# Attention weights turned by VectorE blocks and transfers through DRAM, and memory softmax ahead of the gate

## The chip, the cores and the metric

The kernel runs on one core of a Trainium2 chip. Its metric is the device time of one execution in microseconds (us). The engines named here are TensorE (PE: matmuls and transposes; PEld is its loading of the stationary operand), VectorE (DVE), ScalarE (ACT), GpSimd (POOL) and SyncE (SP). SP and POOL each issue transfers on a queue of their own. SBUF is the memory beside the engines, PSUM the one into which PE writes, DRAM the large memory outside.

## The reference, cut to what matters

Four layers, whose mixers are latent attention, sparse attention, sliding window and latent attention again. Sequence 256, width 2048. Every layer also has four memory heads of dimension 256 over a memory of 256 rows. The part that the change touches is the softmax weight `p` on its way to the product with `v`:

```
def _mla_branch(...):                       # latent: 16 heads, two blocks of 128 queries
    s = (einsum('bqhd,bkhd->bhqk', qn, k_nope) + einsum('bqhd,bkd->bhqk', qr, k_rope)) * scale
    p = softmax(where(causal, s, NEG_INF)); return einsum('bhqk,bkhd->bqhd', p, v)
def _memory_attention(mq, mem_kv):          # 4 heads
    s = einsum('bqhd,bkhd->bhqk', mq, mk) * MEM_HEAD_DIM ** -0.5
    p = softmax(s); return einsum('bhqk,bkhd->bqhd', p, mv)
def reference(...):                         # per layer
    y = concatenate([self_out, mem_out]) * silu(gate)
    x = x + y @ w_out[i]
```

## The kernel before

All products run in fp32r, in two parts: every operand is split into `hi` (a rounded copy, ACT, L65) and `lo` (what is left, DVE, L74), and a product takes three matmuls (hi hi, lo hi, hi lo). Weights come from DRAM by `stage` on SP's queue (L223, and L227 where columns are picked out of each head) into `wr`, a ring of four tiles; `parts_of` splits them in pieces of 128x512 into `wh` and `wl`, rings of four tiles each. `columns_by` puts the features of the result on partitions (L283 with wh, L287 with wl, a piece is 8 matmuls), `rows_by` the rows of the sequence (L263, L264, L265, a piece is 6 matmuls).

A layer works in six parts, in the order 4, 0, 1, 2, 3, 5. Parts 4 and 5 are two memory heads each (`memory_project`, `memory_attend`), the others are self heads; in the two latent layers a part is four heads (`Latent.project`, `Latent.attend`). After the heads of a part come the products of the part before with `w_out` (`acc_wo`, added to `x` by DVE at L1170). So there are 32 latent heads and 16 memory heads in which the changed functions run.

In such a head the scores lie with queries on partitions. DVE and ACT form the softmax `e` (L546 to L552 in latent heads, where L547 shows as ISA in the order: a custom instruction and the reading of its accumulator), ACT multiplies by the reciprocal of the sum (`normalized`). The product with `v` needs keys on partitions: `weights_T` turns `e` in blocks of 128x128 on PE (L524) into the PSUM tile `ptp`, three blocks for a latent head (causal: the upper right one is zero), four for a memory head. `split` makes `pT` hi and lo of it, and L534 and L535 (`attend`) or L612 (`memory_attend`) multiply.

What sets the order: the program is written head after head, and a scheduler with a simulated timeline orders each engine's list when the kernel is built; each engine then runs its list strictly in that order and waits on semaphores. The splits of the weights have a higher priority by 1000 places (`tc.high_priority`). Instructions of the heads stand between those of the surrounding products, so that PE has weights to multiply while DVE and ACT form a softmax. POOL's queue carries the transfers between DRAM and SBUF that aren't weights: `mkr` and `mvr` (keys and values of memory heads), `xm`, the bias tables (`tab`, `bm`) and, towards the end, pieces of `w_out` that are split ahead (`hl`, `sw`, `wk`).

## Time and profile before

| what | value |
|---|---|
| time, median of 3 runs | 2548.99 us (2548.82 to 2549.72) |
| the profiled execution's own time | 2549.14 us |
| its span, first to last instruction | 2547.4 us |
| granted TensorE clock, mean | 0.999 |
| busy: PE / DVE / ACT / POOL | 2534.6 / 1906.2 / 1605.9 / 115.6 us |
| data moved | 515.84 MB, mean 202 GB/s |

The span is what the trace covers, from the first to the last instruction; the time of an execution has a little more around it. Busy shares are averages over the span. Matmul records overlap each other, so a sum of their durations is not PE's time; the distance between starts is. The chain of work is followed back from the last instruction, at each step to what released it. A row of waits gives the engine and line that stood still, what released it, the time in all, the number of times and the longest.

### The profile page before, as it was taken

The page shows a single profiled execution, that of the slowest core. Times are in us where ns is not written, and L with a number is a line of the kernel's source. Part 1 is how long each engine was busy: PE and PEld are TensorE (multiplying, and loading weights), DVE is VectorE, ACT ScalarE, POOL GpSimd, SP SyncE. Part 2 cuts the span into 40 slices and gives each one's busy share as a digit, 9 for nine tenths or more (in the row PEclk, how much of TensorE's full clock was granted, in tenths as well). Part 3 has the DMA queues.
Part 4 walks back from the last instruction along what each step waited for, and adds up shares of the span by engine and source line. Part 5 has one row for each costly group of instructions (what it writes and reads, how often), then busy time and mean ns, then how long its engine had stood idle before and what let it go on. Part 6 is the DMA issues. An engine that isn't in the chain of part 4 may idle for free.

```text
span 2547.4 us, 41829 instructions
## 1 busy us (share of the span) xinstructions
PE 2534.6 (99%) x13928; PEld 2181.2 (86%) x13928; DVE 1906.2 (75%) x4218; ACT 1605.9 (63%) x3480; POOL 115.6 (5%) x274
## 2 busy tenths in 40 slices
PE   9999999999999999999999999999999999999998
PEld 7888888888888889888888888888889888888887
DVE  6666667677777778988787777777878777787776
ACT  6555556566556657667776566766666656665665
POOL 1000000000000000000000010000000000000000
PEclk9999999999999999999999999999999999999999
DMA  8788777666667667666666585666556777676764
GB/s 293 246 266 267 243 218 237 185 166 186 188 175 217 194 203 244 185 201 175 203 182 182 153 258 177 183 177 186 174 172 194 227 205 200 191 194 182 213 180 179
DMA packets 478522, 515.84 MB, mean 202 GB/s; under 512 B 70192, under 2 KB 390592, under 8 KB 477152
## 3 DMA queue, kind: packets, MB, share of 16 engines
q1 hardware_dynamic: 460080, 449.71, 60.6%
q0 software_dynamic: 17504, 62.45, 7.3%
q8 instruction: 110, 1.80, 0.3%
q14 instruction: 108, 0.88, 0.1%
q10 hardware_dynamic: 720, 0.98, 0.1%
HBM read 483.61 MB, written 29.46 MB: 201 GB/s over the span
## 4 chain that ended last, share of the span: by engine, by line
PE 99%; ACT 0%; DVE 0%; DMA 0%; issue 0%; DVEq 0%
PE acc_g L283 14%; PE acc_g L287 7%; PE acc_wo L263 7%; PE acc_wo L264 7%; PE acc_wo L265 7%; PE acc_mq L283 5%; PE acc_q L283 5%; PE acc_mk L283 5%; PE acc_cq L283 4%; PE acc_qn L283 4%; PE acc_mk L287 2%; PE acc_q L287 2%; PE acc_mq L287 2%; PE acc_mv L263 2%; PE acc_mv L264 2%; PE acc_mv L265 2%
## 5 line engine op out<-in xcount | busy, mean ns | idle before, releaser
L74 DVE TENSOR_TENSOR wl<-wr,wh 128x512 fp32r<-128x512 f32 (+1 forms) x1712 | 1154.6, 679 | 545.6 <-ACT wh L65 521.6
L65 ACT ACTIVATE wh<-wr 128x512 fp32r<-128x512 f32 (+1 forms) x1712 | 1060.7, 622 | 775.0 <-PE acc_g L283 160.5
L283 PE MATMUL acc_g<-xT,wh 128*128 128x512 f32 x1536 | 487.3, 397 | 1.1 <-DVE mqT L325 1.1
L287 PEld LDWEIGHTS acc_g<-xT,wl 128*128 128x128 f32 x1536 | 284.0, 188 | 61.7
L287 PE MATMUL acc_g<-xT,wl 128*128 128x256 f32 x1536 | 309.3, 280 | 0.0
L264 PE MATMUL acc_wo<-wl,y 128*128 128x512 f32 x752 | 294.8, 392 | 0.0
L265 PE MATMUL acc_wo<-wh,y 128*128 128x512 f32 x752 | 291.8, 390 | 0.0
L283 PEld LDWEIGHTS acc_g<-xT,wh 128*128 128x128 f32 x1536 | 237.4, 189 | 7.0 <-issue 3.1
L263 PE MATMUL acc_wo<-wh,y 128*128 128x512 f32 x752 | 241.1, 392 | 0.0
L264 PEld LDWEIGHTS acc_wo<-wl,y 128*128 128x128 f32 x752 | 141.3, 188 | 28.8
L265 PEld LDWEIGHTS acc_wo<-wh,y 128*128 128x128 f32 x752 | 141.3, 188 | 28.6
L283 PE MATMUL acc_mq<-xT,wh 128*128 128x512 f32 x512 | 163.1, 397 | 0.0
L263 PEld LDWEIGHTS acc_wo<-wh,y 128*128 128x128 f32 x752 | 139.3, 188 | 27.2 <-ACT wh L65 0.2
L283 PE MATMUL acc_q<-xT,wh 128*128 128x512 f32 x512 | 162.4, 396 | 0.0
L283 PE MATMUL acc_mk<-mT,wh 128*128 128x512 f32 x512 | 161.0, 396 | 0.3 <-ACT wh L65 0.3
L1170 DVE TENSOR_TENSOR x<-x,acc_wo 128x512 f32<-128x512 f32 x184 | 120.6, 680 | 12.0 <-PE acc_wo L265 11.7
L283 PE MATMUL acc_qn<-cT,wh 128*128 128x512 f32 x384 | 121.9, 397 | 0.0
L283 PE MATMUL acc_cq<-xT,wh 128*128 128x512 f32 x384 | 121.0, 396 | 0.0
L287 PEld LDWEIGHTS acc_mk<-mT,wl 128*128 128x128 f32 x512 | 96.0, 188 | 24.1 <-DVE wl L74 1.2
L287 PEld LDWEIGHTS acc_q<-xT,wl 128*128 128x128 f32 x512 | 95.9, 188 | 21.9
L287 PEld LDWEIGHTS acc_mq<-xT,wl 128*128 128x128 f32 x512 | 94.8, 188 | 20.3
L287 PE MATMUL acc_mq<-xT,wl 128*128 128x256 f32 x512 | 103.6, 280 | 0.0
(324 smaller groups left out, 4217.5 us busy)
## 6 DMA issues: line engine op xcount, KB each, us to landing
wr<-in_w_out_dram SPq DMA_DIRECT2D x188, 512.0 KB, 3.7
wr<-in_w_in_a_dram SPq DMA_DIRECT2D x176, 512.0 KB, 4.1
wr<-in_w_mem_kv_dram SPq DMA_DIRECT2D x120, 512.0 KB, 4.8
wr<-in_w_in_b_dram SPq DMA_DIRECT2D x116, 512.0 KB, 3.7
wr<-in_w_in_c_dram SPq DMA_DIRECT2D x104, 512.0 KB, 4.0
wr<-in_w_uq_dram SPq DMA_DIRECT2D x192, 128.0 KB, 2.7
wr<-in_w_uq_dram SPq DMA_DIRECT2D x48, 256.0 KB, 3.4
wr<-in_w_in_a_dram SPq DMA_DIRECT2D x32, 288.0 KB, 3.2
```

Of the source, the lines that this page charges most:

```text
L65: inst = nc.scalar.activation(o, i, AF.Copy, scale=scale)
L74: nc.vector.tensor_sub(lo, src, f32(hi))
L263: nc.tensor.matmul(acc[t][:, :n], xh, wh[:, :n], start=first, stop=False)
L264: nc.tensor.matmul(acc[t][:, :n], xh, wl[:, :n], start=False, stop=False)
L265: nc.tensor.matmul(acc[t][:, :n], xl, wh[:, :n], start=False, stop=last)
L283: nc.tensor.matmul(acc[j], wh[:, o:o + P], q[:, :, kt % 4, :], start=kt == 0, stop=False)
L287: nc.tensor.matmul(acc[j][:, 0, :], wl[:, o:o + P], q[:, 0, kt % 4, :], start=False, stop=kt == kts - 1)
L1170: nc.vector.tensor_add(xs, xs, acc[t])
```

## The change

`weights_T` no longer uses PE. DVE transposes `e` within blocks of 32x32 (one instruction per head, L521, into `tw`). A block transposed in its place still stands in the wrong block row, so four transfers on SP's queue (L527), one for each group of 32 partitions, write `tw` to a DRAM tile `back` with the blocks exchanged: 32 partitions, each with four runs of 96 (latent) or 128 (memory) elements. One transfer on POOL's queue (L528) reads `back` into the SBUF tile `pd`. The splits read `pd` with a stride, since the order within a row is now key first and block second (`by_block`). For 48 heads that is 48 instructions on DVE, 192 transfers on SP's queue of 48 or 64 KB, and 48 on POOL's queue of 192 or 256 KB, in place of 160 transposes on PE.

The scores, the softmax and the turning of the two memory heads move from `memory_attend` into `memory_project`, ahead of the gate's projection. `e` becomes one tile of 128x512 per head (three of them) where it was tiles of 128x256 (four); the other users of that ring (`th`, `cq1`, `rl`, and the two-head softmax of the other mixers) take their part of the larger tile. The room for descriptors of dynamic transfers goes from 8192 to 2048.

```diff
     ...
-    def normalized(e, r, n):
-        copy_act(e[:, :n], e[:, :n], scale=r)
-
-    def weights_T(es, blocks):
-
-        tp = misc("ptp")
-        for i, (b, k) in enumerate(blocks):
-            nc.tensor.transpose(tp[:, i * P:(i + 1) * P], es[b][:, k * P:(k + 1) * P], ident)
-        return tp
+    def weights_T(e, blocks):
+
+        n = blocks * P
+        tw = tmp("tw")[:, :n]
+        nc.vector.transpose(tw.rearrange("p (q b) -> p b q", b=blocks),
+                            e[:, :n].rearrange("p (b q) -> p b q", b=blocks))
+        d = wk.tile([P, 512], F32, name="pd", tag="pd", bufs=2)[:, :n]
+        back = dr.tile([P, 512], F32, name="back", tag="back", bufs=4)[:, :n]
+        to = back.rearrange("(j c) (i x) -> i c j x", c=32, i=4)
+        for i in range(4):
+            nc.sync.dma_start(to[i], tw[32 * i:32 * i + 32].rearrange("c (j x) -> c j x", j=4))
+        nc.gpsimd.dma_start(d, back)
+        return d.rearrange("p (q b) -> p b q", b=blocks)
+
+    def by_block(t, n):
+        return t.rearrange("p (b q) -> p b q", b=n)
 ...
     def masked_softmax(score, bias, scale):
 
-        es = []
+        e = wk.tile([P, 512], F32, name="e", tag="e", bufs=3)
         mn, sm = small("mn", 2), small("sm", 2)
         for b in range(2):
             n = (b + 1) * P
+            u = e[:, b * P:b * P + n]
             sp = score(b)
-            u = wk.tile([P, S], F32, name="u", tag="e", bufs=4)
             bi = bias(b, n)
-            nc.vector.tensor_add(u[:, :n], sp[:, n:2 * n], bi)
-            nc.vector.tensor_tensor_reduce(u[:, :n], sp[:, :n], u[:, :n], -1.0, BIG,
+            nc.vector.tensor_add(u, sp[:, n:2 * n], bi)
+            nc.vector.tensor_tensor_reduce(u, sp[:, :n], u, -1.0, BIG,
                                            op0=OP.add, op1=OP.min, accum_out=mn[:, b:b + 1])
-            e = wk.tile([P, S], F32, name="e", tag="e", bufs=4)
             ms = small("ms", 2)
             nc.vector.tensor_mul(ms[:, :1], mn[:, b:b + 1], scale[0][:, b:b + 1])
-            nc.scalar.activation(e[:, :n], u[:, :n], AF.Exp, bias=ms[:, :1],
+            nc.scalar.activation(u, u, AF.Exp, bias=ms[:, :1],
                                  scale=scale[1][:, b:b + 1], accum_out=sm[:, b:b + 1])
-            es.append(e)
         r = small("rc", 2)
         nc.vector.reciprocal(r, sm)
         for b in range(2):
-            normalized(es[b], r[:, b:b + 1], (b + 1) * P)
-        return weights_T(es, [(0, 0), (1, 0), (1, 1)])
+            copy_act(e[:, b * P:b * 2 * P + P], e[:, b * P:b * 2 * P + P], scale=r[:, b:b + 1])
+        return weights_T(e, 3)
 ...
-        return nm, kT, v, qT, gate(nm, w, g0 + 2048 + part * 512)
-
-    def memory_attend(nm, kT, v, qT, gT):
-        y = act.tile([P, 2, 4, S], F32R, name="y", tag="y", bufs=2)
+        heads = []
         for h in range(2):
-            es = []
+            e = wk.tile([P, 512], F32, name="e", tag="e", bufs=3)
+            e4 = e.rearrange("p (k t q) -> p t k q", k=2, t=2)
             mn, sm = small("mn", 2), small("sm", 2)
             for b in range(2):
                 sp = misc("msp")
@@ -592,17 +595,23 @@
                 nc.vector.tensor_reduce(mn[:, b:b + 1], sp[:, :S], AX.X, OP.max, negate=True)
                 ms = small("ms", 2)
                 nc.vector.tensor_mul(ms[:, :1], mn[:, b:b + 1], nm.col("rstd", b))
-                e = wk.tile([P, S], F32, name="e", tag="e", bufs=4)
-                nc.scalar.activation(e, sp[:, :S], AF.Exp, bias=ms[:, :1], scale=nm.col("rstd", b),
-                                     accum_out=sm[:, b:b + 1])
-                es.append(e)
+                nc.scalar.activation(e4[:, b], by_block(sp[:, :S], 2), AF.Exp, bias=ms[:, :1],
+                                     scale=nm.col("rstd", b), accum_out=sm[:, b:b + 1])
+            heads.append((e, e4, sm))
+        tps = []
+        for e, e4, sm in heads:
             r = small("rc", 2)
             nc.vector.reciprocal(r, sm)
             for b in range(2):
-                normalized(es[b], r[:, b:b + 1], S)
-            tp = weights_T(es, [(0, 0), (1, 0), (0, 1), (1, 1)])
+                copy_act(e4[:, b], e4[:, b], scale=r[:, b:b + 1])
+            tps.append(weights_T(e, 4))
+        return v, tps, gate(nm, w, g0 + 2048 + part * 512)
+
+    def memory_attend(v, tps, gT):
         y = act.tile([P, 2, 4, S], F32R, name="y", tag="y", bufs=2)
+            split(by_block(pH, 4), by_block(pL, 4), tps[h])
 ...
-                split(pT[0], pT[1], tp[:, :S])
-                copy_act(pT[2], tp[:, S:S + P])
+                split(by_block(pT[0], 2), by_block(pT[1], 2), tp[:, :2])
+                copy_act(pT[2], tp[:, 2])
 ...
-                     dynamic_dma_scratch_size=8192)
+                     dynamic_dma_scratch_size=2048)
```

PE, around the softmax of the first latent head in the first layer; `acc_wo` are the products of the part before, `acc_qn` the next part's projection, `o` the head's product with `v`, `sp` the next scores. Before:

```order
L264 MATMUL acc_wo_6688<-wl,y 128x512
L265 MATMUL acc_wo_6688<-wh,y 128x512
L264 MATMUL acc_wo_6689<-wl,y 128x512
L265 MATMUL acc_wo_6689<-wh,y 128x512
L524 MATMUL ptp<-ident,e 128x128 x3
L263 MATMUL acc_wo_6688<-wh,y 128x512
L263 MATMUL acc_wo_6689<-wh,y 128x512
L263 MATMUL acc_wo_6736<-wh,y 128x512
L263 MATMUL acc_wo_6737<-wh,y 128x512
```

After, where that head's product with `v` begins:

```order
L287 MATMUL acc_qn_6800<-cT_3840,wl 128x256
L287 MATMUL acc_qn_6801<-cT_3840,wl 128x256
L283 MATMUL acc_qn_6800<-cT_3840,wh 128x512
L283 MATMUL acc_qn_6801<-cT_3840,wh 128x512
L287 MATMUL acc_qn_6800<-cT_3840,wl 128x256
L287 MATMUL acc_qn_6801<-cT_3840,wl 128x256
L541 MATMUL o<-pT,va 128x256
L748 MATMUL sp<-kn,qn 128x256
L749 MATMUL sp<-kr,qrT 128x256
L541 MATMUL o<-pT,va 128x256 x2
L542 MATMUL o<-pf,vf 128x128
L750 MATMUL sp<-kn,qn 128x128
```

The row of three transposes is gone, and the head's product with `v` (L541 after, L534 before), which stood 20 products of `acc_wo` behind the transposes, now stands among the pieces of `acc_qn`, behind all products of that `w_out`.

DVE at the same head, from the reciprocal of the sum (`rc`) to the low part of the turned weights (`pT`); `x_72` and `x_73` are the residual's tiles. Before:

```order
L556 RECIPROCAL rc<-sm 128x2
L1170 TENSOR_TENSOR x_72<-x_72,acc_wo_6640 128x512
L1170 TENSOR_TENSOR x_73<-x_73,acc_wo_6641 128x512
L74 TENSOR_TENSOR wl<-wr,wh 128x512 x4
L74 TENSOR_TENSOR pT<-ptp,pT 128x256
L1170 TENSOR_TENSOR x_72<-x_72,acc_wo_6688 128x512
L1170 TENSOR_TENSOR x_73<-x_73,acc_wo_6689 128x512
L74 TENSOR_TENSOR wl<-wr,wh 128x512 x3
```

After:

```order
L561 RECIPROCAL rc<-sm 128x2
L74 TENSOR_TENSOR wl<-wr,wh 128x512
L1179 TENSOR_TENSOR x_72<-x_72,acc_wo_6654 128x512
L1179 TENSOR_TENSOR x_73<-x_73,acc_wo_6655 128x512
L521 STREAM_TRANSPOSE tw<-e 128x3x128
L74 TENSOR_TENSOR wl<-wr,wh 128x512 x4
L1179 TENSOR_TENSOR x_72<-x_72,acc_wo_6702 128x512
L1179 TENSOR_TENSOR x_73<-x_73,acc_wo_6703 128x512
L74 TENSOR_TENSOR wl<-wr,wh 128x512 x2
L74 TENSOR_TENSOR pT<-pd,pT 128x256
L74 TENSOR_TENSOR wl<-wr,wh 128x512 x2
```

The transpose `tw` has come in, and between it and the split from `pd` stand six splits of weights and two additions, where before four splits and two additions stood between the reciprocal and the split from `ptp`.

SP, the weight loads from the first `w_out` to the gate of the part of latent heads that follows; `uq` and `ukv` are the projections of the latent, `in_a` the layer's input projection (here the gate's columns). Before:

```order
L223 DMA wr<-in_w_out_dram 128x2x512 x8
L227 DMA wr<-in_w_uq_dram 128x2x128 x24
L227 DMA wr<-in_w_ukv_dram 128x2x128 x8
L227 DMA wr<-in_w_ukv_dram 128x4x128 x4
L223 DMA wr<-in_w_in_a_dram 128x4x256 x8
```

After:

```order
L223 DMA wr<-in_w_out_dram 128x2x512 x8
L227 DMA wr<-in_w_uq_dram 128x2x128 x4
L527 DMA back<-tw 32x4x96 x4
L227 DMA wr<-in_w_uq_dram 128x2x128 x20
L227 DMA wr<-in_w_ukv_dram 128x2x128 x4
L527 DMA back<-tw 32x4x96 x4
L227 DMA wr<-in_w_ukv_dram 128x2x128 x4
L227 DMA wr<-in_w_ukv_dram 128x4x128 x4
L223 DMA wr<-in_w_in_a_dram 128x4x256
L527 DMA back<-tw 32x4x96 x4
L223 DMA wr<-in_w_in_a_dram 128x4x256 x5
L527 DMA back<-tw 32x4x96 x4
```

Among the loads of one part there now stand four groups of four transfers `back<-tw`, one for each head.

## Rows read from the trace of the kernel before

**Rows 1.** Page, parts 1 and 4: busy us, share, instructions; the chain by engine.

```profile
PE 2534.6 (99%) x13928; PEld 2181.2 (86%) x13928; DVE 1906.2 (75%) x4218; ACT 1605.9 (63%) x3480; POOL 115.6 (5%) x274
...
PE 99%; ACT 0%; DVE 0%; DMA 0%; issue 0%; DVEq 0%
```

**Rows 2.** Waits of PE, first and last of seven rows: us in total, times, longest.

```profile
PE wu L107 <- DVE ones L103: 1.1, 1, 1.1
...
PE acc_va L263 <- DVE ms L551: 0.2, 1, 0.2
```

**Rows 3.** Tile `ptp`: instructions of one line, duration in ns as min/median/max.

```profile
L524 PE MATMUL ptp<-ident,e x160: 269/272/273, 515.0 to 2515.0; 128*128 128x128 f32 x160
```

**Rows 4.** Timeline of PE, latent head of layer 0: start us, us, instruction, count.

```profile
843.05 1.07 PE L263 MATMUL acc_wo<-wh,y 128*128 128x512 f32 x4
843.96 0.39 PE L264 MATMUL acc_wo<-wl,y 128*128 128x512 f32 x1
...
848.50 0.49 PE L524 MATMUL ptp<-ident,e 128*128 128x128 f32 x3
848.74 1.17 PE L263 MATMUL acc_wo<-wh,y 128*128 128x512 f32 x4
849.75 0.40 PE L264 MATMUL acc_wo<-wl,y 128*128 128x512 f32 x1
```

**Rows 5.** Timeline of PE, memory head of the last layer.

```profile
2497.17 0.62 PE L263 MATMUL acc_wo<-wh,y 128*128 128x512 f32 x2
...
2498.53 0.62 PE L263 MATMUL acc_wo<-wh,y 128*128 128x512 f32 x2
2498.99 0.60 PE L524 MATMUL ptp<-ident,e 128*128 128x128 f32 x4
...
2500.36 1.11 PE L263 MATMUL acc_wo<-wh,y 128*128 128x512 f32 x4
```

**Rows 6.** Timeline of DVE, same stretch; in brackets idle before and releaser.

```profile
861.99 0.69 DVE L74 TENSOR_TENSOR wl<-wr,wh 128x512 fp32r<-128x512 f32 x1 [0.70 <-ACT wh L65]
863.38 0.69 DVE L74 TENSOR_TENSOR wl<-wr,wh 128x512 fp32r<-128x512 f32 x1 [0.70 <-ACT wh L65]
...
864.19 0.42 DVE L74 TENSOR_TENSOR pT<-ptp,pT 128x256 fp32r<-128x256 f32 x1
```

**Rows 7.** Timeline of ACT, same stretch as rows 6.

```profile
861.33 0.63 ACT L65 ACTIVATE wh<-wr 128x512 fp32r<-128x512 f32 x1 [0.76 <-PE acc_mq L283]
862.72 0.63 ACT L65 ACTIVATE wh<-wr 128x512 fp32r<-128x512 f32 x1 [0.76 <-PE acc_mq L283]
863.52 0.39 ACT L65 ACTIVATE pT<-ptp 128x256 fp32r<-128x256 f32 x1 [0.17 <-PE ptp L524]
```

**Rows 8.** Tile `wr`: issues on SP, duration in ns as min/median/max.

```profile
L227 SPq DMA_DIRECT2D wr<-in_w_uq_dram x240: 367/467/2017, 491.5 to 2363.9; - x120
...
L223 SPq DMA_DIRECT2D wr<-in_w_out_dram x188: 367/368/368, 564.4 to 2512.2; - x188
```

**Rows 9.** Waits of ACT on a weight load.

```profile
ACT wh L65 <- DMA wr<-in_w_uq_dram: 11.9, 17, 0.9
```

**Rows 10.** DMA issues: queue, count, KB each, median us from issue to landing.

```profile
wr<-in_w_out_dram SPq DMA_DIRECT2D x188, 512.0 KB, 3.7
...
wr<-in_w_ukv_dram SPq DMA_DIRECT2D x64, 128.0 KB, 2.6
...
xm<-x POOLq DMA_DIRECT2D x24, 256.0 KB, 3.0
...
bm<-tab POOLq DMA_DIRECT2D x32, 128.0 KB, 4.5
...
hl<-in_w_out_dram POOLq DMA_DIRECT2D x16, 128.0 KB, 3.7
...
out_dram<-xg SPq DMA_DIRECT2D x1, 128.0 KB, 1.9
```

**Rows 11.** Page, part 5: busy us, mean ns; idle before and what ended it.

```profile
L74 DVE TENSOR_TENSOR wl<-wr,wh 128x512 fp32r<-128x512 f32 (+1 forms) x1712 | 1154.6, 679 | 545.6 <-ACT wh L65 521.6
```

More of the change, by code (lines that the diff above doesn't have):

```diff
@@ L503, in gate @@
                 nc.vector.tensor_mul(hz, z, nm.half)
-                th = wk.tile([P, S], F32, name="th", tag="e", bufs=4)
+                th = wk.tile([P, 512], F32, name="th", tag="e", bufs=3)[:, :S]
                 nc.scalar.activation(th, hz, AF.Tanh)
@@ L601, in memory_attend @@
             for b in range(2):
-                normalized(es[b], r[:, b:b + 1], S)
-            tp = weights_T(es, [(0, 0), (1, 0), (0, 1), (1, 1)])
+                copy_act(e4[:, b], e4[:, b], scale=r[:, b:b + 1])
+            tps.append(weights_T(e, 4))
+        return v, tps, gate(nm, w, g0 + 2048 + part * 512)
+    def memory_attend(v, tps, gT):
+        y = act.tile([P, 2, 4, S], F32R, name="y", tag="y", bufs=2)
+        for h in range(2):
             pH, pL = (wk.tile([P, 768], F32R, name="pT", tag="pT", bufs=PT)[:, :512] for z in range(2))
-            split(pH, pL, tp)
+            split(by_block(pH, 4), by_block(pL, 4), tps[h])
             o = misc("mo")
@@ L670, in first @@
                     z = total(acc[m])
-                    s1 = sq if n == 0 else wk.tile([P, S], F32, name="cq1", tag="e", bufs=4)
+                    s1 = sq if n == 0 else wk.tile([P, 512], F32, name="cq1", tag="e", bufs=3)[:, :S]
                     nc.scalar.activation(s1, z, AF.Square)
@@ L844, in selection @@
                     sp = misc("isp")
-                    rl = wk.tile([P, S], F32, name="rl", tag="e", bufs=4)
+                    rl = wk.tile([P, 512], F32, name="rl", tag="e", bufs=3)[:, :S]
                     if b == 0:
@@ L955, in head_pair @@
             mn, sm = small("mn", 4), small("sm", 4)
-            both = wk.tile([P, S], F32, name="u", tag="e", bufs=4)
-            one = wk.tile([P, S], F32, name="u", tag="e", bufs=4)
-            last = wk.tile([P, S], F32, name="u", tag="e", bufs=4)
+            two = wk.tile([P, 512], F32, name="u", tag="e", bufs=3)
+            both, one = two[:, :S], two[:, S:]
+            last = wk.tile([P, 512], F32, name="u", tag="e", bufs=3)[:, :S]
             if swa:
```

## The prediction, made before the changed kernel was run

> **What bounds the kernel now.** I read the page's busy times and its chain first. The reader is to see that PE is busy for 2534.6 of 2547.4 us and that the chain that ended last is PE for 99% of the span [rows 1]. Then the waits of PE: seven rows, the longest wait 1.1 us, together 4.9 us [rows 2]. So the kernel lasts as long as PE's list of matmuls. What shortens that list at an unchanged pace shortens the run, and what makes PE wait lengthens it; work on DVE, ACT, the queues and POOL counts only through such waits. The profiled execution took 2549.14 us, 0.15 above the median of 2548.99, with 1.7 us outside its span; I make the sum against 2549.14 and do not correct for so little.
>
> **What is removed.** 160 transposes at L524 (32 latent heads of three, 16 memory heads of four) leave PE. Each record lasts 0.272 us [rows 3], but PE overlaps its records, so I take the price from starts. Around a latent head of layer 0, four L263 matmuls take 0.91 us from the first start to the start of L264; where three transposes stand ahead of the same four, the way from the first transpose to L264 is 849.75 - 848.50 = 1.25 us [rows 4]. Three transposes thus cost 0.34, 0.115 each. In a memory head of the last layer, the period from one pair of L263 to the next is 1.36 us, and 2500.36 - 2498.53 = 1.83 with four transposes in it [rows 5]: 0.47, or 0.1175 each. At their mean 0.1165, 160 x 0.1165 = **18.6 us**; at 0.11 and 0.12 it is 17.6 and 19.2. No other matmul goes or comes.
>
> The Trainium skill ("TensorE: Matmul & The Clock Gate", Part 4: PE-mode transpose) says that a full transpose took about 275 ns inside one kernel. The trace agrees as to the record's length, 0.272 us, and not as to what one costs the engine. By the page the sum would lose 160 x 0.275 = 44 us, an estimate, instead of 18.6; its result, priced by the record's own row, is rival D.
>
> **What is added.** A head now needs one transpose in blocks on DVE, four transfers on SP's queue to DRAM, one on POOL's queue back into `pd`, and the same two splits as before, from `pd` in place of PSUM. None of these is in the trace of before.
>
> *DVE.* The nearest rows to the block transpose are additions of 128x256 at 0.42 us and of 128x512 at 0.69 us [rows 6]. Between them I put 0.56 for 384 columns and take 0.69 for 512: 32 x 0.56 + 16 x 0.69 = 29 us, from 22 (0.42 and 0.56) to 33 (all at 0.69). It does not lie on the path: in the pieces of weights DVE idles 0.70 us in each 1.39 [rows 6], and ACT waits 0.76 for PE's release of a buffer [rows 7]. What hides it is the ring of four wh and wl tiles. A copy starts when PE leaves the tile four back, wl is ready 1.35 us later (861.33 to 862.68), and PE gets there after three pieces, 4.17 us: 2.8 us ahead. One transpose takes 0.7 of that at most and the idle time of the next piece gives it back. Were the cover gone, it would cost up to 29 us: rival C. Strided splits from `pd` I price like those of before, 0.42 on DVE and 0.39 on ACT [rows 6, 7]; both stand in that same slack.
>
> *The queues.* On SP the four transfers stand between weight loads. Their wait for the transpose is no new one, since the load queued behind them waits for a later row of DVE anyway; what is left is 4 issues of 0.37 to 0.47 us [rows 8], up to 1.9 per head, by which weights start later. The loads mostly lie ready when ACT wants them: for those of `uq`, the most waited for, it waits 17 times, 11.9 us in all, never over 0.9 [rows 9]. So I take nothing, with up to 0.4 per head as the other end (rival B). On POOL's queue the transfer back is followed by other transfers and holds no engine but POOL, 5% busy [rows 1]. The smaller descriptor room I take at nothing; its price can only be that of a later `pd`, which is rival A's.
>
> *The new wait.* Before, the transposes and the splits were done a few us after the softmax. Now PE's first matmul on the weights (L541, or L594 in memory heads) comes only after the trip. If the trip is longer than the room the order leaves, `pT<-pd,pT` on DVE and the copy on ACT stop, the wl and wh splits queued behind them stop too, and PE runs out of tiles. So I compare trip and room.
>
> Trip, from the end of the transpose: three further SP issues, 3 x 0.37 = 1.1 (the first counts in its landing); landing in DRAM 2.6, the row of a 128 KB load on SP, between 1.9 (128 KB written at the end) and 3.7 (512 KB); landing in `pd` 3.7, the row of 128 KB on POOL, between 3.0 (256 KB) and 4.5 (128 KB) [rows 10]; ACT's copy 0.39 [rows 7]. Sum 7.8. Hand-overs between engines and queueing behind a 512 KB load (3.7 - 2.6 = 1.1 at most) I put at 1.0, the least certain term: **8.8 us**, with ends 7.2 (1.1 + 1.9 + 3.0 + 0.4 and 0.8) and 11.0 (1.1 + 3.7 + 4.5 + 0.4 and 1.3).
>
> Room, from the order after the change, by the pace of before. Example: the first latent head of a layer's first part. From the piece whose wl was made last ahead of `tw` to L541 stand 36 matmuls of acc_wo and 8 of acc_qn: 36 x 0.2275 (0.91 / 4, [rows 4]) + 1.39 [rows 6] = 9.6 us; plus DVE's lead 2.8, less two x additions ahead of `tw` 1.4 and `tw` itself 0.55: 10.5 us. Tightest is the last latent head of each latent layer: four pieces of 1.39 and two matmuls, 6.0, + 2.8 - 0.1 - 0.55 = 8.2. Counted so, and scaled by some 3% to meet the span, the 48 rooms run from 8.2 to 22 us with a median of 10.7; nine are under 9.3, fourteen under 9.8, twenty under 10.3. The shortfalls, summed over heads, are 0 at a trip of 7.8, 1.2 us at 8.8, 9.0 at 9.8, 17 at 10.3, 28 at 10.8, 57 at 11.8. I take the mean over 7.8, 8.8 and 9.8, as trips will scatter by about 1 us: **3.4 us**.
>
> **The sum.** 2549.1 - 18.6 + 3.4 = **2533.9 us**.
>
> **The rivals.** *A, slower: the trip is longer than the room.* One mechanism: `pd` comes late, DVE and ACT hold the weight splits behind it, PE idles. It breaks even at a trip of about 10.4 us, where the shortfalls reach 18.6; at 10.8 the time is 2549.1 - 18.6 + 28 = 2558.5. For it: the trip's upper end is 11.0, and `bm` shows that 128 KB can take 4.5 on POOL's queue [rows 10]. Against it: the middle rows give 8.8, and the loss counts each shortfall in full though a lead once lost does not shorten later rooms. The Trainium skill ("DMA: Bandwidth & Descriptors", the specifications) says that runs below 512 B are read, changed and written back; latent heads write runs of 384 B. No row here shows what that costs; it speaks for A.
>
> *B, no gain: the 192 issues and the turns of the queue delay weights.* If of the up to 1.9 us per head that loads start later some 0.4 reached PE at each head, 48 x 0.4 = 19 us would be back: 2549. For it: the 17 waits on `uq` loads. Against it: so few waits in so many loads, 0.9 us at the longest, though a load of `w_out` takes 3.7 us to land [rows 10].
>
> *C, no gain: DVE sets the pace.* If two thirds of its 29 us came onto the path, 19 us, the result is again 2549. For it: DVE is at 75%. Against it: 545.6 us of its idle time stand before the wl splits alone [rows 11].
>
> *D, a larger gain: a transpose is worth its whole record.* 160 x 0.272 = 43.5, so 2549.1 - 43.5 + 3.4 = 2509. Against it: the starts in [rows 4, 5].
>
> **How the numbers follow.** Forecast 0.73, A 0.13, B 0.06, C 0.05, D 0.03. The forecast's own range is 2549.1 - 19.2 = 2530 with no shortfall and 2549.1 - 17.6 + 9 = 2540.5 with a trip of 9.8. To leave out no more than 2 in 10 the range goes on to B and C and a trip near the point of balance: 2529.5 to 2547. 0.2% is 5.1 us, about what a measurement of this kernel can tell from no change. Faster takes the forecast and D, 0.76; B and C, 0.11, lie within; A, 0.13, is slower.
>
> **What would show it.** The price of the transposes: no rows of L524, PE's busy time about 18 us lower, and four L263 in 0.91 us through a softmax. The trip: the landings of `back` and `pd`, and rows in which ACT or DVE wait for `pd`. The room: waits of PE for `pT` or, at L541 and L594, for ACT; none above 1 us if I am right, and at the last head of a latent layer first. DVE's price: the mean of its transposes against 0.56 and 0.69. SP: ACT's waits for weight loads, 12 us from `uq` now. The prediction would be wrong if `pd` is ready only 10 us or more after `tw`, or if PE's waits for wh and wl grow in the parts with attention heads.

## The result, and the profile after

The changed kernel takes 2569.02 us, median of four runs (2567.64 to 2572.67), against 2549.35 for the kernel before in the same comparison: a ratio of 1.0077, with a 95% interval of 1.0065 to 1.0089. It is slower by 20 us, where I had forecast 15 us less. Its profiled execution took 2567.64 us, with a span of 2565.9.

The first thing to look at is the page's busy times, to be read beside [rows 1].

```profile
PE 2528.2 (99%) x13768; PEld 2167.0 (84%) x13768; DVE 1931.6 (75%) x4266; ACT 1606.7 (63%) x3480; POOL 141.0 (5%) x322
```

The 160 transposes are gone from PE (13768 matmuls for 13928), and PE is busy for 6.4 us less although the span grew by 18.5. So PE now stands still for longer; the page's shares don't show it, since 99% is 99% in both. The waits do. Of PE (engine, line, what released it: us in total, times, longest), the first three rows, where [rows 2] had 1.1 at the top:

```profile
PE mo L621 <- ACT pT L65: 5.4, 3, 3.5
PE o L541 <- ACT pT L65: 4.9, 4, 3.4
PE acc_kn L283 <- ACT kn L65: 4.5, 4, 1.1
```

All rows of this view add up to 29.6 us, 4.9 before. Of these three only the first two name the turned weights. The third names `kn`, a copy out of an accumulator that has nothing to do with them. The cause stands in the same view of ACT and of DVE:

```profile
ACT pT L65 <- DMA pd<-back: 99.1, 42, 5.9
...
ACT hl L1153 <- DMA hl<-in_w_out_dram: 12.3, 5, 3.9
```

```profile
DVE pT L74 <- ACT pT L65: 89.3, 41, 5.8
```

In 42 of 48 heads ACT reaches its copy from `pd` before `pd` is there, and stands still for 2.4 us on average; DVE stands still behind it. The tiles of the new instructions say what they cost (duration in ns as min/median/max; taken by shape, a transpose is 0.70 us at the mean with 384 columns and 1.10 with 512):

```profile
L521 DVE STREAM_TRANSPOSE tw<-e x48: 691/707/1126, 492.1 to 2508.1; 128x384 f32<-128x384 f32 x32, 128x512 f32<-128x512 f32 x16
```

```profile
L65 ACT ACTIVATE pT<-pd x48: 538/548/1157, 500.3 to 2529.4; 128x256 fp32r<-128x256 f32 x32, 128x512 fp32r<-128x512 f32 x16
L74 DVE TENSOR_TENSOR pT<-pd,pT x48: 497/508/1112, 501.4 to 2530.7; 128x256 fp32r<-128x256 f32 x32, 128x512 fp32r<-128x512 f32 x16
```

And the transfers, beside [rows 10] (KB each, median us to landing):

```profile
back<-tw SPq DMA_DIRECT2D x128, 48.0 KB, 2.0
pd<-back POOLq DMA_DIRECT2D x32, 192.0 KB, 3.9
...
back<-tw SPq DMA_DIRECT2D x64, 64.0 KB, 1.8
...
pd<-back POOLq DMA_DIRECT2D x16, 256.0 KB, 5.3
```

From the end of the block transpose to the landing of `pd`, taken head by head from the trace, the trip is 8.3 us at the median in latent heads (6.6 to 11.3) and 9.7 in memory heads (7.1 to 17.2).

**One head, followed.** The second latent head of the first layer loses time at a place where its own product is not late. ACT, PE and then ACT again, from the timelines (start us, us, instruction, in brackets the idle time before it and what ended it):

```profile
612.58 1.14 ACT L65 ACTIVATE wh<-wr 128x512 fp32r<-128x512 f32 x2
616.28 0.54 ACT L65 ACTIVATE pT<-pd 128x256 fp32r<-128x256 f32 x1 [2.56 <-DMA pd<-back]
616.72 0.36 ACT L65 ACTIVATE pf<-pd 128x128 f32<-128x128 f32 x1
616.98 1.66 ACT L65 ACTIVATE wh<-wr 128x512 fp32r<-128x512 f32 x3
...
622.25 0.64 ACT L65 ACTIVATE kn<-acc_kn 128x256 fp32r<-128x256 f32 x2
```

```profile
617.38 0.28 PE L541 MATMUL o<-pT,va 128*128 128x256 f32 x1
...
621.46 0.40 PE L287 MATMUL acc_kn<-cT,wl 128*128 128x256 f32 x2
623.00 0.47 PE L283 MATMUL acc_kn<-cT,wh 128*128 128x512 f32 x1 [1.15 <-ACT kn L65]
```

ACT waits 2.56 us for `pd`. PE takes up the product (L541) at 617.38 with no wait: by that alone the head would have been in time. But ACT has lost 2.56 us, makes up three weight splits in a row, and comes to the copy `kn` only at 622.25; PE, which needs that accumulator, stands from 621.9 to 623.0. The delay reaches PE 5 us later and under another name. In e13, e15, e17 and e18 below, in which little or nothing is waited for, PE has no such wait for `kn`'s copy.

**The largest stall, and what follows it.** In the memory heads at the end of the first layer ACT waits 5.73 us, and PE has nothing left:

```profile
923.72 1.11 ACT L65 ACTIVATE pT<-pd 128x512 fp32r<-128x512 f32 x1 [5.73 <-DMA pd<-back]
```

```profile
920.81 0.61 PE L263 MATMUL acc_wo<-wh,y 128*128 128x512 f32 x2
924.88 0.58 PE L621 MATMUL mo<-pT,mvr 128*128 128x256 f32 x1 [3.45 <-ACT pT L65]
925.26 0.63 PE L264 MATMUL acc_wo<-wl,y 128*128 128x512 f32 x1
925.68 0.63 PE L265 MATMUL acc_wo<-wh,y 128*128 128x512 f32 x1
```

The stretches of 2 us around it (us, busy us of PE, PEld, DVE, ACT and POOL with counts, then TensorE's granted clock, DMA share, GB/s):

```profile
922.00:924.00 2.00, 0.00 (x0) 0.00 (x0) 0.00 (x0) 0.28 (x1) 0.00 (x0) 1.00 1.02 401
924.00:926.00 2.00, 1.12 (x3) 1.03 (x4) 1.14 (x2) 2.00 (x4) 0.00 (x0) 0.65 0.95 400
926.00:928.00 2.00, 2.00 (x6) 1.52 (x6) 2.00 (x3) 1.96 (x3) 0.00 (x0) 0.50 0.09 34
```

Behind a stretch in which PE did nothing the granted clock falls to 0.50 of 2.4 GHz, that is to 1.2 GHz, and matmuls start 0.42 us apart instead of 0.23. At 0.65 and 0.50 over 2 us each, this takes 0.7 + 1.0 = 1.7 us on top of the stall. The same happens once more, in the second layer, behind two shorter waits of PE at `mo` (1.5 and 0.7 us).

### The profile page after: what moved, and what is told of

It reads as the page before. It is cut to its first block, busy times and chain, and to the rows that moved or that the text cites. A ratio compares the mean times of both kernels' runs of the same rounds, so it can differ in the third digit from the quotient of the medians.

```text
span 2565.9 us, 41985 instructions
## 1 busy us (share of the span) xinstructions
PE 2528.2 (99%) x13768; PEld 2167.0 (84%) x13768; DVE 1931.6 (75%) x4266; ACT 1606.7 (63%) x3480; POOL 141.0 (5%) x322
## 5 line engine op out<-in xcount | busy, mean ns | idle before, releaser
L65 ACT ACTIVATE wh<-wr 128x512 fp32r<-128x512 f32 (+1 forms) x1712 | 1049.2, 621 | 685.9 <-PE acc_wo L265 114.1
L283 PEld LDWEIGHTS acc_g<-xT,wh 128*128 128x128 f32 x1536 | 239.5, 189 | 11.9 <-ACT vf L65 2.6
```

Source lines behind the costliest of these rows:

```text
L65: inst = nc.scalar.activation(o, i, AF.Copy, scale=scale)
L283: nc.tensor.matmul(acc[j], wh[:, o:o + P], q[:, :, kt % 4, :], start=kt == 0, stop=False)
```

## The experiments

Each time below is a median, with the ratio to the kernel before in the same comparison. Several views compare the kernels by stretches: I took from each trace the start of the first `acc_wo` matmul of every part and subtracted that of before; what a stretch gains or loses is the difference of two neighbours.

Five theories stood against each other. **1**: the trip is waited for, and ACT and DVE lose what they stand still. **2**: DVE and ACT have too much to do. **3**: the transfers delay the weights. **4**: the memory softmax ahead of the gate costs. **5**: the splits and products of the heads now stand at a worse place in the order, wait or no wait. e1, e2, e13, e15, e17 and e18 leave out the exchange of blocks, and e3 the turning as a whole; they are there for their time alone.

**Taking parts away (e1 to e4).**

```diff
 # e1: nobody waits for the transfers (tw takes pd's ring, and pd that of tw)
-        return d.rearrange("p (q b) -> p b q", b=blocks)
+        return tw.rearrange("p (q b) -> p b q", b=blocks)
 # e2: as e1, and without these
-        for i in range(4):
-            nc.sync.dma_start(to[i], tw[32 * i:32 * i + 32].rearrange(...))
-        nc.gpsimd.dma_start(d, back)
 # e3: neither transpose nor transfers
+        return e[:, :n].rearrange("p (q b) -> p b q", b=blocks)
 # e4: weights_T on PE, memory splits ahead of the gate
+        for i in range(blocks):
+            nc.tensor.transpose(tp[:, i * P:(i + 1) * P], e[:, i * P:(i + 1) * P], ident)
```

> As the changed kernel, but the splits read the blocks that DVE turned (tw), which lie in SBUF already; the four transfers to DRAM and the one back still run, and nothing waits for them. The weights then keep the wrong block order, so that part of the computation is changed. Theory 1 (the trip is waited for: ACT stands 99 us for pd, and PE's tiles and accumulators come late behind it): the wait goes, so 2549 - 18.6 for the transposes and a few us of what is left, 2530 to 2536. Theory 2 (DVE and ACT have too much to do: 48 block transposes of 0.71 or 1.11 us and strided splits that take 0.54 to 1.12 instead of 0.39 to 0.60): all of that is still there, so 2555 to 2569. Theory 3 (the transfers delay the weights on SP's queue and in the DMA engines): still there too, 2555 to 2569.

> As the changed kernel, but without the transfers to DRAM and back; the splits read the turned blocks (tw) from SBUF, in the wrong block order. Theory 1 (the wait for the trip): the same as with transfers that nobody waits for, 2530 to 2536. Theory 2 (work of DVE and ACT): 2555 to 2569. Theory 3 (traffic and issues): 2530 to 2536 here, and 20 us or more above that with the transfers left in.

> As the changed kernel, but the weights are not turned at all: no block transpose on DVE, no transfers, the splits read e itself with the same stride, in memory heads right behind the softmax. This leaves out the turning. It gives the price of the 160 transposes on PE with nothing in their place: 2549 - 18.6 = 2530.5 by my price of 0.1165 us each; 2505 if each were worth its record of 0.272. Theory 2 (work of DVE and ACT): 2530, clearly under the kernel that has DVE's transposes and no transfers. Theories 1 and 3: within 3 us of that one.

> The other part of the change alone: one e tile per head, memory scores, softmax and splits ahead of the gate's projection, but the weights turned by PE into PSUM as before. Theories 1 to 3: this part costs nothing, 2545 to 2552. Theory 4 (the earlier memory softmax and the smaller number of e tiles hold DVE, ACT and POOL up): 2560 or more.

Measured: e1 2536.0 us (0.9944, 0.9929 to 0.9959), e2 2533.9 (0.9935, 0.9920 to 0.9950), e3 2535.0 (0.9941, 0.9924 to 0.9957), e4 2549.8 (1.0001, 0.9991 to 1.0010). Theory 4 falls with e4. Theory 2 falls with e2 and e3: with DVE's 48 transposes and without them the time is the same. Theory 3 has at most the 2 us between e1 and e2, which lie within their intervals, as long as the splits stand early. Without the wait, 33 us are gone. And e3 gives the price of the transposes with nothing in their place: 2549.7 - 2535.0 = 14.7 us, 0.092 each, where I had 0.1165. Its interval is 11 to 19 us, so my 18.6 is not excluded.

**One class of heads (e5, e6).** In e5 `memory_project` turns on PE as in e4 and only latent heads take the new way; in e6 it is the other way round.

> The 32 latent heads go by DVE and DRAM, the 16 memory heads by PE (softmax and splits still ahead of the gate). 96 transposes fewer on PE: 11 us. In the trace of the changed kernel the latent parts of the first and last layer are 18 us behind the kernel in which nobody waits for the transfers, the stretches with memory heads 14 us. If each head brings its own loss: 2549.7 - 11 + 18 = 2557 (2552 to 2560). Rival (memory heads and latent heads disturb each other on POOL's queue, and the loss needs both): 2545 or less.

> The 16 memory heads go by DVE and DRAM, the 32 latent heads by PE. 64 transposes fewer on PE: 7.5 us. If each head brings its own loss, 14 us in the stretches with memory heads: 2549.7 - 7.5 + 14 = 2556 (2552 to 2560). Rival (the loss needs both): 2545 or less.

e5: 2564.8 us (1.0061, 1.0046 to 1.0076). e6: 2549.7 (0.9998, 0.9988 to 1.0007). I had the losses too even. Latent heads alone are 15 us slower, so they lose 26 beside the 11 that I gave their transposes (23 if a transpose is worth 0.092); memory heads alone come out even, although ACT waits 30.0 us for `pd` there, against 76.7 in e5.

**More room by order (e7 to e11).** I tied ACT's copies from `pd`, by a rule of order that adds no wait, to a place behind a later split of weights; `made` lists these splits, `turned` and `ahead` the copies `pT` and `pf`.

```diff
 # e7: pT in latent heads, 3 weight splits later; e9: pT and pf
+    for ins, n in zip(turned, BEHIND):
+        if n:
+            tc.add_manual_dep(ins, made[n].name, ...NoSync...)
 # e8 (9, 12), e10 and e11 (13, 15): memory heads behind these splits of the w_out that follows
+            with tc.issue_after(made[at + (13, 15)[h]]) if at else ExitStack():
                 split(by_block(pH, 4), by_block(pL, 4), tps[h])
```

In the latent heads e8 is as e7 and e10 as e9; in e11 they turn on PE.

> As the changed kernel, with one more rule of order: in latent heads ACT's copy from pd stands behind the third weight split that followed it so far, about 4 us more room between the block transpose and the splits from pd. Nothing else differs. Theory 1 (the trip is longer than the room, and what stands behind the waiting copy comes late too): most of the 18 us of the latent parts go, 2569 - 15 = 2554 (2550 to 2558). Theory 1a (only PE's waits at the product itself count, 5 us at o in the trace): 2563 or more. Theory 2 (work of DVE and ACT): no change, 2566 to 2571.

> As the kernel with more room in latent heads, and the memory heads of each layer's last part take their splits from pd only behind the tenth and thirteenth weight split of the output projection that follows, where they took them near its first third. Theory 1: the waits of PE at mo and the stretch at the lower clock behind them go too, another 8 to 12 us: 2540 to 2546, faster than the kernel before by 4 to 9 us. Theory 1a: 2555 or more. Theory 2: 2566 or more.

> The kernel with more room in latent heads left one reader of pd, the copy pf, where it was, and ACT waited for pd at that copy 44 us. Here both copies from pd stand three weight splits later on ACT; nothing else differs from the changed kernel. Theory 1 (the loss comes from ACT and DVE standing still for pd): the trip of about 9 us has 4 us more room, most of the latent heads' loss goes, 2569 - 15 = 2554 (2548 to 2559). Theory 5 (what costs is that the product comes late after the softmax at all, through the tiles that the head holds, and not the standing still): 2565 or more.

> As the kernel with both copies from pd three weight splits later in latent heads, and the memory heads of each layer's last part take their splits only behind the 14th and 16th weight split of the output projection. Theory 1: 2541 to 2549. Theory 5: 2558 or more.

> Latent heads by PE, memory heads by DVE and DRAM, with the splits from pd in each layer's last part behind the 14th and 16th weight split of the output projection that follows. Theory 1: the 7 us that were lost with memory heads alone come back, 2549.7 - 7 = 2543 (2540 to 2546), faster than the kernel before. Theory 5: 2549 or more.

None of it brought the time back. e7: 2584.6 (1.0135, 1.0120 to 1.0150) and e8: 2577.6 (1.0107, 1.0092 to 1.0122), both worse: I had left the copy `pf` where it was, and it became the one that stands still.

```profile
ACT pf L66 <- DMA pd<-back: 44.0, 19, 4.2
ACT pT L66 <- DMA pd<-back: 43.7, 22, 5.6
```

With both copies tied, e9 takes 2570.4 (1.0082, 1.0067 to 1.0097), e10 2566.3 (1.0066, 1.0051 to 1.0081). By what I had expected, both come out for theory 5. In e9 the waits for `pd` halve, but not the time:

```profile
ACT pT L66 <- DMA pd<-back: 48.7, 28, 5.6
```

Two things spoil it as a test. The tie moved the transposes too: from `tw` to the split from `pd` there are 9, 7, 5 and 8 weight splits in the first part's heads, where it was 6, 5, 5 and 7, so the room grew by three, two, none and one, not by three each. And one stretch, part 1 of the last layer, got worse by itself, 11.0 us behind the kernel before where the changed kernel is 5.7 (below, e14). e11, memory heads alone with more room, is 2552.8 (1.0013, 1.0003 to 1.0022), a miss too: its loss is in the last part of the last layer (4.6 us, against a gain of 3.2 in e6), where nothing follows that could hide a later product. So order alone did not settle between 1 and 5.

**One step instead of two (e12).**

```diff
-        (four transfers to back, one from it)
+        for k in range(16):
+            i, j = k // 4, k % 4
+            q = nc.gpsimd if k % 8 in (2, 5, 7) else nc.sync
+            q.dma_start(d[32 * j:32 * j + 32, i * m:i * m + m], tw[32 * i:32 * i + 32, j * m:j * m + m])
```

> As the changed kernel, but the blocks go from tw to pd in one step, within SBUF: 16 transfers of one block row each per head, ten on SP's queue, six on POOL's. By the issues (10 x 0.37 us on SP, 6 x 0.54 us on POOL) and a landing of 2 to 2.7 us the trip is 5.7 to 6.2 us instead of 8.4, with about the same room in the order. Theory 1: most of the 33 us go, 2536 to 2546. Theory 5 (the room itself costs): 2560 or more. Theory 3 (768 transfers on the queues hold weights up): 2560 or more, with waits of ACT for weight loads.

2613.0 us (1.0244, 1.0227 to 1.0261): theory 3, which had no part in e1 and e2, at three times the dose. An issue on SP lasts 0.59 us here, not 0.37, so ten of them hold the queue for about 6 us while weights wait behind them:

```profile
L528 SPq DMA_DIRECT2D pd<-tw x480: 507/588/1726, 493.5 to 2570.7; - x160
```

```profile
ACT pT L65 <- DMA pd<-tw: 79.3, 38, 5.3
ACT wh L65 <- DMA wr<-in_w_in_a_dram: 21.0, 18, 3.2
ACT wh L65 <- DMA wr<-in_w_uq_dram: 13.7, 24, 1.1
ACT wh L65 <- DMA wr<-in_w_ukv_dram: 12.7, 19, 4.5
```

The trip was no shorter for it, and ACT now waited for weights as well ([rows 9] had 11.9 us at most for one kind). What it shows is that rival B's mechanism exists at ten issues on SP per head; at four, e1 and e2 can tell none. A part of the 64 us is the clock: the mean granted clock of its runs is 0.989 to 0.991, that of the kernel before 0.999, and 0.008 of 2613 us, about 20 us as an estimate, goes with it.

**The same places, another wait (e13, e15 to e18).** This is the test that the order experiments were meant to be: each of the 48 pairs of splits is tied to the number of weight splits that it has ahead of it in the changed kernel, and what it waits for differs. The splits stand where they stood in all five kernels, to one split; the transposes moved ahead by up to six weight splits in e13 and e15, in which nothing waits for their transfers, by at most two in e17 and e18, and not at all in e16.

```diff
 # all: BEHIND = the places in the changed kernel, for pT and pf alike
 # e13: reads tw, transfers run      # e15: reads tw, no transfers
 # e16: nothing else (control)
 # e17
-        for i in range(4):
-            nc.sync.dma_start(to[i], tw[32 * i:32 * i + 32].rearrange("c (j x) -> c j x", j=4))
+        nc.sync.dma_start(back, tw)
 # e18
+        nc.gpsimd.dma_start(d, tw)     # instead of the way through back
```

> The kernel in which the splits read tw while all transfers run and nobody waits for them, but with all 48 pairs of splits tied to the places on ACT that they have in the changed kernel (the same number of weight splits ahead of each). The weights keep the wrong block order. Theory 1 (ACT and DVE standing still for pd costs the time): 2534 to 2542, as with the early splits. Theory 5 (the late place among the short projections costs it): 2555 to 2569. Between the two, each has its share.

> As the kernel with the splits from tw at the changed kernel's places, without any transfer to DRAM and back. Theory 1: 2533 to 2541. Theory 5: 2553 to 2567. Theory 3 (issues and traffic, in the late places): 5 us or more below the same kernel with transfers.

> The changed kernel with its own places of the splits tied down, nothing else: a control for the tying. 2567 to 2572 by every theory.

> The splits at the changed kernel's places; one transfer writes tw to DRAM as it lies, instead of four that exchange the blocks, and one reads it back (wrong block order in the weights). Three issues of 0.4 us fewer, so the trip is about 7.2 us from the end of the block transpose to the landing instead of 8.4, and 144 transfers fewer stand on SP's queue. Theory 1 (ACT's room in this order is about 6.3 us, the mean start of its copy without the wait; what the trip is longer stops ACT and DVE): the waits of ACT for pd fall from 99 us to about half, 2553 to 2561. Theory 5 (the late place costs): 2565 to 2570. Theory 3 (SP's issues hold weights up): 2560 or more.

> The splits at the changed kernel's places; a single transfer on POOL's queue copies tw to pd within SBUF, with nothing in DRAM and nothing on SP's queue (wrong block order). The trip is about 3.5 us, well inside ACT's room. Theory 1: hardly any wait for pd, 2537 to 2545. Theory 5: 2553 or more.

| kernel | trip, median us (latent heads) | ACT's waits for `pd`, us | time, us | ratio and interval |
|---|---|---|---|---|
| e16, five transfers (control) | 8.0 | 99.5 | 2567.7 | 1.0074, 1.0059 to 1.0089 |
| e17, two transfers | 6.7 | 39.4 | 2548.1 | 0.9990, 0.9981 to 1.0000 |
| e18, one transfer | 3.4 | 0.4 | 2544.1 | 0.9975, 0.9965 to 0.9984 |
| e13, transfers run, nothing waits | not waited for | none | 2545.3 | 0.9981, 0.9972 to 0.9990 |
| e15, no transfers | none | none | 2537.3 | 0.9952, 0.9937 to 0.9966 |

```profile
ACT pT L66 <- DMA pd<-back: 99.5, 43, 6.2
```

```profile
ACT pT L66 <- DMA pd<-back: 39.4, 26, 4.2
```

```profile
ACT pT L66 <- DMA pd<-tw: 0.4, 1, 0.4
```

These are e16, e17 and e18. Theory 1 has most of it: at unchanged places, 23 us hang on the wait (2567.7 or 2569.0 against 2545.3). PE's own waits go the same way: 29.6 us in the changed kernel, 26.9 in e16, 13.7 in e17, 10.1 in e18, 11.8 in e13, 8.6 in e15. Theory 5 has at most the 3.4 us between e2 and e15, which lie within their intervals. e13 came out 3 us above what I had expected by theory 1, for which the transfers' share (next) would do. And the dependence is bent: the first 39 us of ACT's waits cost about 4 us of time, the next 60 cost 20. e17 came out faster than I had expected, 2548 for 2553 to 2561, because I had drawn the line straight. It has 144 issues fewer on SP as well; but e13 has all of them and is faster still, so they are not what it gained.

**POOL's queue (e14).** Between e13 and e15 lie 8 us that are transfers without a wait. In the stretch of part 1 of the last layer, the kernels with `pd` of latent heads on POOL's queue and the splits at the late places lose (changed kernel 5.7 us, e13 2.9, e17 4.7, e18 5.0), and e15 loses 0.4. What is there: `split_ahead` works on the last output weights, with a ring of two tiles `hl`, and its transfers are tied to program order on POOL. In the changed kernel, POOL's timeline shows them behind four `pd`, which wait for their `back` (the third, by its row, for DVE):

```profile
2186.04 0.54 POOL L528 DMA_DIRECT2D pd<-back  x1 [32.88 <-DMA back<-tw]
2202.91 0.54 POOL L528 DMA_DIRECT2D pd<-back  x1 [16.34 <-DMA back<-tw]
2215.30 0.54 POOL L528 DMA_DIRECT2D pd<-back  x1 [11.85 <-DVE wl L74]
2232.34 0.54 POOL L528 DMA_DIRECT2D pd<-back  x1 [16.50 <-DMA back<-tw]
2232.87 0.55 POOL L1157 DMA_DIRECT2D sw<-hl  x1
2240.12 0.54 POOL L1143 DMA_DIRECT2D hl<-in_w_out_dram  x1 [6.71 <-DMA sw<-hl]
```

and ACT pays when they come all at once:

```profile
2243.82 0.42 ACT L1153 ACTIVATE hl<-hl 128x256 fp32r<-128x256 f32 x1 [3.14 <-DMA hl<-in_w_out_dram]
...
2253.24 0.42 ACT L1153 ACTIVATE hl<-hl 128x256 fp32r<-128x256 f32 x1 [3.94 <-DMA hl<-in_w_out_dram]
```

In the kernel before ACT never waits for `hl` from DRAM. e14 takes the tie away:

```diff
-            pin(nc.gpsimd.dma_start(f32(q)[:, 1, :], w[k * P:(k + 1) * P, c0:c0 + S]))
+            nc.gpsimd.dma_start(f32(q)[:, 1, :], w[k * P:(k + 1) * P, c0:c0 + S])
-            pin(nc.gpsimd.dma_start(split_w[n // 4][:, n % 4], q))
+            nc.gpsimd.dma_start(split_w[n // 4][:, n % 4], q)
```

> The changed kernel, in which the 32 transfers hl and sw, which split the last part's output weights ahead in layer 3, are no longer tied to program order on POOL, so that they stand between the pd transfers and not behind four of them. The splits stand where they stood. In the changed kernel the stretch of layer 3 that has them is 4.9 us behind the same stretch of layer 0. If that is the burst of late hl: 2569 - 5 = 2564 (2562 to 2566). If not: 2567 to 2571.

The waits for `hl` are gone, and the stretch loses 0.5 us instead of 5.7. The time isn't better, 2571.9 (1.0072, 1.0050 to 1.0095). Its four runs lie apart, and they go with the clock: 2561.1 us at a mean granted clock of 0.997, 2571.1 at 0.996, 2572.8 at 0.995, 2575.4 at 0.994. As an estimate, 0.003 of 2570 us is some 8 of the 14 us between them. The last is the profiled one; it gave the gain back elsewhere, among other places in a stall of 3.7 us at another latent head's product, in the next part.

So e14 doesn't show that `hl` cost the 5.7 us. In that stretch of the changed kernel PE itself waits 4.4 us behind late `pd` (3.4 at a product, 1.1 at `kn`) and 0.9 for weight splits, which a late `hl` can delay; in e14 that product was not late. The better measure is e13, e17 and e18, where no wait of PE in the stretch names `pd`: they lose 2.5 to 4.6 us more there than e15. And e1, whose splits stand early, has ACT waiting 10.4 us for `hl` and loses nothing in the stretch (it gains 1.5 us, e2 gains 1.4), so late `hl` costs only together with the late places.

## Why the prediction was wrong, point by point

*The bound* was read rightly: PE's list sets the time, and what PE waits sets most of the rest (29.6 us for 4.9).

*The transposes* were priced about rightly: 18.6 us predicted, 14.7 measured in e3 (11 to 19), where PE's busy time falls by 17.4; in e2 that falls by 14.5. Whether they were overpriced is not shown. Three of them in 0.34 us are 0.113 each, not 0.115, which is worth 0.2 us in the sum. Rival D is out: the record of 0.272 is not what a transpose costs.

*DVE's work* was mis-sized and hidden, as said: 0.70 and 1.10 us for 0.56 and 0.69, strided copies of 0.54 for 0.39, some 40 us for 29 on the transposes alone; e2 and e3 show that it costs nothing. Rival C is out.

*The trip* was right as a sum: 8.8 us with ACT's copy, that is 8.4 to the landing, and 8.4 is the median over all heads. That the terms cancel is luck: at the median `back` landed in 1.8 us for 2.6, `pd` in 4.2 for 3.7, the three issues took 1.3 for 1.1, and the hand-over from `back` to POOL 0.6 for 1.0 with the queueing. What was missing is the spread, 6.6 to 11.7 us in 46 heads. In the last two it is 16.6 and 17.2, but their copies stand so late that they wait for nothing. The Trainium skill's remark on runs under 512 B ("DMA: Bandwidth & Descriptors", the specifications) shows little here: 48 KB in runs of 384 B land in 2.0 us, 64 KB in runs of 512 B in 1.8, so 0.2 us more for less data.

*The room* is the step that failed. I measured it to PE's first product and let the lead of DVE, 2.8 us, count in full as room: 10.7 us at the median, and only the shortfall beyond it as a loss, 3.4 us in all. As PE's room that count was good: in e18, where next to nothing waits, PE's first product starts 10.5 us behind the transpose at the median, in e15 10.7. But the instruction that waits is ACT's copy, and ACT comes to it earlier, in e18 6.5 us behind the transpose. In the changed kernel the copy starts 8.4 us behind it at the median, of which 2.1 on average (99.1 / 48) are waiting, so ACT's own room is some 6.3 (taken head by head, 6.0 at the median). In 42 of 48 heads the trip is longer than the head's own room. I had written that ACT, DVE and the splits behind them stop; I then priced the stop as if the lead that it eats were free. It isn't: the lead is what covers every other copy and split behind it, among them evacuations like `kn` that PE waits for within a few us. By e13, e16 and the changed kernel the wait costs 22 to 24 us at 8.4 to the landing, where my table of shortfalls (8.8 with ACT's copy) has 1.2, and at 7.0 (e17, all heads) 3 to 4, where it has none. Rival A was the right mechanism with the wrong balance: I put it at a trip of 10.4, and by e17 it lies near 7.4, counted the same way. My own sign of being wrong, `pd` ready only 10 us or more after `tw`, rested on the same room and did not show at the median. The other did: PE waited up to 3.5 us for ACT's `pT`, where I had none above 1, and longest at a memory head (their product is L621; the L594 of the prediction is their score product).

*The queues.* On SP four issues per head cost nothing that e1 and e2 can tell, as said. On POOL I wrote that the transfer back "holds no engine but POOL". It held the `hl` and `sw` behind it, and through them ACT: 2.5 to 4.6 us in one stretch by e13, e17 and e18 against e15. The prediction has no term for that.

*The sum, with what was measured in place of each term*: 2549.7 - 14.7 (transposes, e3) - 1.1 (e2 against e3, within the intervals) + 3.4 (later places, e15 against e2, within the intervals) + 8.0 (transfers, POOL's queue the largest part that I found, e13 against e15) + 23.7 (the wait, changed kernel against e13) = 2569.0. The terms come from different comparisons, whose intervals are 4 to 8 us wide each; only the sign of the first and the rough size of the last are beyond doubt. A part of the last is the clock's: 6.8 us of the changed kernel and 10.2 of e16 pass at 1.2 GHz before the program's end, none of e13, which is 3 to 5 us at half the pace.

**What stays open.** Whether the heads could be given enough room by order: my ties moved the transposes along. Of the 8 us between e13 and e15 the two profiled executions show 4.3, of which 2.5 lie in the stretch above and 2.2 in the last part; the rest is not placed. The smaller room for descriptors stands in all these kernels, also in e4, which takes the time of before; what it does to the landing of `pd` no run here separates. No kernel here that computes the reference was faster than the kernel before by more than its interval.

## What to carry to other kernels

A wait is priced at the engine that executes it, in its own order, and not at the engine that needs the result: ask where that engine would be without the wait, and count every instant that it stands still against the lead that covers all it does next. A slack that one late transfer may use up is no slack for 48 of them. And before a transfer is added to a queue, look at what is tied behind it there, even on that of an engine that is 5% busy.

## What the runs showed of the hardware that I had not expected

- SP's issue of a small transfer between partitions of SBUF (32 partitions, 12 or 16 KB, e12) took 0.59 us at the median, longer than that of 512 KB of weights, 0.37 ([rows 8]).
- A strided copy of 128x512 from SBUF took 1.12 us on ACT and 1.09 on DVE at the mean; the same split from PSUM, read along the row, took at most 0.60 and 0.69.
- A block transpose of 128x384 took 0.70 us and one of 128x512 1.10 us at the mean, more than in proportion to the columns (1.33 times the columns, 1.6 times the time).
- PE's idle stretch of 3.45 us was followed by 3.4 us at 1.2 GHz, 1.7 us of further loss. Not every stretch was: the one of 3.35 us at another product of the changed kernel (at 2295 us) was not, one of 2.4 us in e17 (at 2242) was.
